# The values of an mLSTM as seven half-depth products, and which work fills which stage

## The chip, the cores and the metric

The kernel runs on one core of one Trainium2 chip. The metric is the device time of one execution in microseconds (us). A profile is one further execution, recorded by the hardware profiler; its times are us from the first instruction. The engines are TensorE (PE; its weight loads are PEld), VectorE (DVE), ScalarE (ACT), GpSimd (POOL) and SyncE (SP), which issues most DMAs.

## The reference, cut to what matters

One block of a model: x is 1024 rows of 1024 numbers, all arithmetic in float32. `h` is the normed x, and one big projection of it gives everything else.

```python
h = rmsnorm(x, norm_g[layer])
proj = jnp.einsum('bsd,de->bse', h, w_in[layer])
(a_q, a_k, a_v, a_o, a_z, a_g, b_q, b_k, b_v, b_z, g_a, g_b) = jnp.split(proj, _split_points(), axis=-1)
...
y_a = hm * jax.nn.sigmoid(a_o) * jax.nn.silu(a_z)
...
y_b = att.reshape(B, S, DA_WIDTH).astype(x.dtype) * jax.nn.silu(b_z)
mix = (jax.nn.sigmoid(g_a + gb[0]) * jnp.einsum('bsc,cd->bsd', y_a, w_branch_a[layer])
       + jax.nn.sigmoid(g_b + gb[1]) * jnp.einsum('bsc,cd->bsd', y_b, w_branch_b[layer]))
x = x + jnp.einsum('bsd,de->bse', mix, w_out[layer])
```

Each part of `proj` is 1024 wide, but for a_g, which is 16. `hm` comes from an mLSTM over four heads of 256 (q and k go through a short convolution and silu, the values a_v directly), run forward and backward. `att` is an attention over eight heads of 128, each the difference of two softmaxes.

## The kernel before, in words

**Precision.** Every product is made of float32r matmuls of split operands: each operand is a rounded high part H and the rest L, and HxH, HxL and LxH are summed, three matmuls per slice of 128 of the depth. For a weight block, `load_w` (L177) loads 512 KB into a `raw` tile (two of them), ScalarE copies it to `wH` (L204), and GpSimd subtracts to get `wL` (L209, or in eight pieces at L207 during the opening and the mLSTM). `run` (L386) lets these loads go ahead of use as far as six half-size weight slots allow.

**Pairs.** Two column blocks of w_in are multiplied together with Strassen-Winograd's scheme: seven products of half the depth in place of eight. The row combinations of h (`TH`, `TL`) are made once in the opening. `load_form` (L230) makes the seven combinations of weight quarters, `pair_units` (L270) the products, each with 512 columns moving and 12 matmuls; products 0, 1, 2 and 6 collect in bank X, 3 and 5 in G, 4 in F, and a `sink` takes each finished quarter. Sixteen pairs are done so: q and k of the mLSTM (`conv_sink`), and o and z of the mLSTM (`oz_sink`). The order in `build` lets product 6 and 5 of one pair stand among products 0, 3, 1, 4, 2 of the next. Large tiles of this stage are called `big` (six buffers), among them `cin`, `y` and `oz`; `tz` has two buffers.

**Units and filling.** Work is a list of units, each with a planned cost; `Weaver.weave` interleaves lists by cost and by the due times in `LAG`. TensorE's order is exactly that list (`keep(E.PE)`); behind the opening the other engines' and SP's instructions are placed by a scheduler. A gate (ga or gb, 16 blocks of 128 columns, each 48 matmuls in 16 units) depends on nothing and is used to fill: `fill(m)` takes the next m gates, and `gate_units` (L831) stores each finished half (tanh, L837, then a DMA to `tga` or `tgb`).

**Stages.**
1. Opening: x is loaded, normed and transposed; four gates fill.
2. The sixteen pairs.
3. Attention: for each of eight heads q and k with a rope (`da_proj`, L842), the head's z, and for two heads at once the values (`da_v`, L892, by `v_units`, L436). Scores of one of eight row blocks take two score tiles (L923); VectorE reduces each (L926), ScalarE takes the exponential (L928), VectorE combines them (L934); then transposes, the product with the values and a norm. `FILL` gives gates to heads 0 and 7. Three gates stand behind it.
4. mLSTM (`ml_head`, `ml_units` L1239): chunks of 256 rows, both directions. The values of head n+1 are projected by `v_units` as filler while head n runs, 32 units of six matmuls each; the first head's values stand ahead of it, the last head is filled with gates.
5. Behind the mLSTM `rest` holds the gates that are left. Five units of it go first, then the last outputs of the mLSTM (`late`) with some more, then loads of y of the attention (`load_y`, L1310: DMA to `yraw`, two buffers, ScalarE copy, VectorE subtraction, tile `sl_yb`) woven into what remains.
6. Products with w_branch_b (L1339), w_branch_a (L1341), then w_out (L1399).

The lines that set these counts:

```python
FILL = (1, 0, 0, 0, 0, 0, 0, 3)
...
ml, late = self.ml_units([self.ml_head(n, stm[n]) for n in range(NH_A)], fill(2))
...
rest = fill(len(gq))
cut = len(rest) // 4
w.add(*rest[:5])
w.weave(late, rest[5:cut])
```

Of the kernel before, what the change touches and what calls it, by code (L numbers as in the profile page):

```python
# [14 lines left out]
S = 1024  # L15
# [22 lines left out]
FILL = (1, 0, 0, 0, 0, 0, 0, 3)  # L38
# [71 lines left out]
class Block:  # L110
# [66 lines left out]
    def load_w(self, key, nxt=None):  # L177
# [3 lines left out]
        if key[0] == "sw":  # L181
            return self.load_form(key)
        wH = self.wpool.tile([128, 8, 128], F32R, name="wH", tag="wH")
# [35 lines left out]
    def pair_raws(self, p):  # L219
        if p >= len(self.pairs) or p in self.praws:  # L220
            return
        self.praws[p] = raws = []
        for seg, i in self.pairs[p]:
# [4 lines left out]
            raws.append(t)  # L228

    def load_form(self, key):  # L230
# [18 lines left out]
        elif f == 2:  # L249
            src = tmp("s3f")  # L250
            sub(src, r1[:, lo], r2[:, lo])
        elif f == 3:
            self.s1f = src = tmp("s1f")
# [16 lines left out]
    def pair_units(self, p, sink):  # L270
# [37 lines left out]
        return [[Unit(6 * MM, lambda f=f, k0=k0: product(f, k0), (("sw", p, f),)) for k0 in (0, 2)] for f in range(7)]  # L308

# [76 lines left out]
    def run(self, units):  # L386
# [10 lines left out]
        for i, u in enumerate(units):  # L397
            if u.keys:
# [4 lines left out]
                while nxt < len(order) and (order[nxt] in self.loaded or not self.opening  # L403
                                            and (order[nxt][0] != "sw" or hasattr(self, "_s0")) and ahead(order[nxt])):
# [436 lines left out]

    def da_proj(self, h, st):  # L842
# [44 lines left out]
        z = self.proj(kz, 0, lambda ps: zz(0, ps)) + self.proj(kz, 1, lambda ps: zz(1, ps), name=("z", h))  # L887
        for half in range(2):
            z[(half + 1) * self.PIECES - 1].after = ((("G", h - 1, half), LAG["G"]),)
# [138 lines left out]
    def ml_head(self, n, st):  # L1028
# [24 lines left out]
        def vv(c, ps):  # L1053


# [4 lines left out]
            a.copy(H[:, :, 0:DH], ps)  # L1060
            low(Lo[:, :, 0:DH], ps, H[:, :, 0:DH])
# [161 lines left out]
        def out(i, half):  # L1223
            ps = self.bank("T")
            for k in range(4):
# [8 lines left out]
                    v=self.v_units("av", n, vv, order=(3, 2, 1, 0)), weigh=step(weigh),  # L1234
# [4 lines left out]
    def ml_units(self, heads, gates):  # L1239
# [5 lines left out]
        av = list(x["v"])  # L1245
        take = lambda n: [av.pop(0) for _ in range(n)]
        for c in (3, 2, 1, 0):
            un += x["k"](c)
        for c in range(NC):
            un += x["gb"](c) + x["HL"](c)  # L1250
        un += take(12) + x["weigh"](3, 1) + take(4) + x["state"](3, 1)
        un += x["weigh"](2, 1) + take(6) + x["state"](2, 1)
        un += x["weigh"](1, 1) + take(6) + x["state"](1, 1) + x["split"](0)
        un += take(4) + x["S"](0) + gates[0:8]
        gates = gates[8:]
        prev = None
        for n, x in enumerate(heads):
            nx = heads[n + 1] if n + 1 < len(heads) else None
            if nx:
                other, share = list(nx["v"]), ((3, 3), (2, 1), (2, 2), (3, 3), (2, 2), (1, 2), (2, 1), (2, 1))  # L1260
            else:
                other, share = gates, ((2, 2), (1, 1), (2, 1), (2, 1), (2, 1), (2, 1), (2, 0), (1, 0))
            for t in range(8):
# [37 lines left out]
                if nx:  # L1301
                    un += {1: nx["k"](3) + nx["gb"](0), 2: nx["k"](0) + nx["k"](2) + nx["HL"](0), 3: nx["k"](1) + nx["gb"](1),
                           4: nx["HL"](1), 5: nx["gb"](2), 6: nx["HL"](2), 7: nx["gb"](3) + nx["HL"](3)}.get(t, [])
# [125 lines left out]
    def build(self):  # L1429
# [21 lines left out]
        with pool(name="const", bufs=1) as self.const, \  # L1451
# [20 lines left out]
            self.pairs, sinks, self.praws, self.f = [], [], {}, {}  # L1472
            for n in range(NH_A):
                for i, seg in enumerate(("ak", "aq")):
# [3 lines left out]
                    sinks.append(self.oz_sink(2 * n + i))  # L1478
            self.ident = self.const.tile([128, 128], F32, name="ident")
# [27 lines left out]
            g0, g1, g2, g3 = (fill(1) for _ in range(4))  # L1507
# [28 lines left out]
            products = [self.pair_units(i, sinks[i]) for i in range(len(self.pairs))]  # L1536
# [31 lines left out]
            ml, late = self.ml_units([self.ml_head(n, stm[n]) for n in range(NH_A)], fill(2))  # L1568
# [72 lines left out]
```

## Time and profile before

| | |
|---|---|
| Runs, median of 3 | 1688.82 us |
| Runs, lowest and highest | 1687.5 and 1688.95 us |
| Profiled execution, first to last instruction | 1685.6 us |
| Matmuls in the profile, transposes among them | 9431 |
| DMA over the span | 178.79 MB, 106 GB/s |
| Stage 1, 2, 3 (from, us) | 0, 71, 398 |
| Stage 4, 5, 6 (from, us) | 1108, 1377, 1413 |

The profiled execution's own time is its span, 3.2 us under the median of the runs. In the profile a group's mean duration of a matmul includes its passage through the array, so that matmuls overlap; what one costs in a stream is the spacing, the length of an unbroken stretch over the matmuls in it. A row with "<-" names who ended a wait. A row ending in q (SPq) is an engine's sequencer issuing.

### The profile page before, as it was taken

How to read it: one execution, taken by the hardware profiler on the slowest of the kernel's cores; microseconds unless marked ns; L12 is line 12 of the kernel's file. 1: busy time of each engine (PE TensorE's matmuls, PEld its weight loads, DVE VectorE, ACT ScalarE, POOL GpSimd, SP SyncE). 2: the span in 40 equal slices, each digit the busy share in tenths (PEclk: the TensorE clock that was granted, in tenths of full speed). 3: DMA queues.
4: the chain of work that ended last, by engine and by line, in shares of the span. 5: the costliest groups of instructions: out<-in, count | busy, mean ns of one | idle time of the engine just before them, and what ended most of it. 6: DMA issues, size and time to landing. Idle time of an engine off the chain costs nothing. (4 is left out here: it accounts for less than half of the span.)

```text
span 1685.6 us, 25370 instructions
## 1 busy us (share of the span) xinstructions
PE 1645.8 (98%) x9431; PEld 1385.3 (82%) x9431; DVE 992.4 (59%) x1799; ACT 760.3 (45%) x1522; POOL 635.2 (38%) x712
## 2 busy tenths in 40 slices
PE   7999999999999999999999999999999999999998
PEld 5777887887877988898888888899999877888887
DVE  5778678675286766666666665325666754135533
ACT  7454555553255454444445445334655644122221
POOL 5767676655343334333451332122322412212000
PEclk9999999999999999999999999999999999999999
DMA  5334434434231213211322222166455337344222
GB/s 180 101 117 137 138 113 137 126 125 127 74 80 48 74 38 88 51 51 39 100 59 56 62 58 70 57 181 176 144 160 161 89 117 244 126 149 126 88 93 83
DMA packets 175630, 178.79 MB, mean 106 GB/s; under 512 B 12185, under 2 KB 135410, under 8 KB 175506
## 3 DMA queue, kind: packets, MB, share of 16 engines
q1 hardware_dynamic: 174594, 175.58, 34.8%
q8 instruction: 74, 1.21, 0.3%
q10 hardware_dynamic: 912, 1.59, 0.2%
q14 instruction: 50, 0.41, 0.1%
HBM read 114.11 MB, written 46.24 MB: 95 GB/s over the span
## 5 line engine op out<-in xcount | busy, mean ns | idle before, releaser
L429 PE MATMUL pj<-hH,wH 128*128 128x512 f32 x640 | 265.8, 415 | 3.3 <-ACT f L542 1.5
L429 PE MATMUL pj<-hH,wL 128*128 128x512 f32 x640 | 251.3, 393 | 1.8 <-POOL wL L207 1.8
L429 PE MATMUL pj<-hL,wH 128*128 128x512 f32 x640 | 250.1, 391 | 0.2 <-DVE hL L580 0.2
L209 POOL TENSOR_TENSOR wL<-raw,wH 128x1024 fp32r<-128x1024 f32 x41 | 99.7, 2432 | 278.0 <-ACT wH L204 268.3
L928 ACT ACTIVATE e<-S,nm 128x1024 f32<-128x1024 f32 x128 | 142.7, 1115 | 134.1 <-DVE nm L926 133.9
L948 DVE TENSOR_TENSOR pL<-T,pH 128x512 fp32r<-128x512 f32 x128 | 87.9, 688 | 117.4 <-ACT pH L947 116.7
L926 DVE TENSOR_REDUCE nm<-S 128x1 f32<-128x1024 f32 x128 | 150.5, 1217 | 10.1 <-PE S L923 9.3
L451 PE MATMUL pj<-wH,hH 128*128 128x256 f32 x512 | 149.9, 293 | 1.6 <-DVE vL L1035 1.4
L429 PEld LDWEIGHTS pj<-hH,wH 128*128 128x128 f32 x640 | 120.4, 188 | 37.7 <-issue 14.1
L451 PE MATMUL pj<-wL,hH 128*128 128x256 f32 x512 | 144.9, 283 | 1.4 <-POOL wL L207 1.4
L429 PEld LDWEIGHTS pj<-hH,wL 128*128 128x128 f32 x640 | 120.1, 188 | 30.2 <-POOL wL L207 3.4
L451 PE MATMUL pj<-wH,hL 128*128 128x256 f32 x512 | 144.5, 282 | 0.0
L429 PEld LDWEIGHTS pj<-hL,wH 128*128 128x128 f32 x640 | 120.7, 189 | 18.2 <-DVE hL L580 0.6
L429 PE MATMUL pj<-sl_yb,wH 128*128 128x512 f32 x384 | 118.9, 390 | 2.1 <-DVE sl_mb L1339 1.6
L947 ACT CAST pH<-T 128x512 fp32r<-128x512 f32 x128 | 74.7, 584 | 100.5 <-PE T L131 99.8
L204 ACT CAST wH<-raw 128x1024 fp32r<-128x1024 f32 x56 | 58.8, 1050 | 114.7 <-PE pj L429 75.8
L923 PE MATMUL S<-kst,qq 64*128 64x512 f32 x768 | 106.5, 408 | 0.0
L451 PEld LDWEIGHTS pj<-wH,hH 128*128 128x128 f32 x512 | 97.7, 191 | 6.8 <-issue 3.9
L451 PEld LDWEIGHTS pj<-wL,hH 128*128 128x128 f32 x512 | 97.5, 190 | 2.3 <-POOL wL L207 2.3
L451 PEld LDWEIGHTS pj<-wH,hL 128*128 128x128 f32 x512 | 97.7, 191 | 0.1
L934 DVE SCALAR_TENSOR_TENSOR e<-e,r,e 128x1024 f32<-128x1024 f32 x64 | 88.9, 1389 | 2.2
L923 PEld LDWEIGHTS S<-kst,qq 64*128 64x128 f32 x768 | 67.8, 184 | 26.2 <-issue 10.5
(358 smaller groups left out, 4101.4 us busy)
## 6 DMA issues: line engine op xcount, KB each, us to landing
raw<-in_w_in_dram SPq DMA_DIRECT2D x88, 512.0 KB, 3.9
kst<-hl SPq DMA_DIRECT2D x64, 128.0 KB, 2.4
qq<-hl SPq DMA_DIRECT2D x64, 128.0 KB, 2.4
x<-in_x_dram SPq DMA_DIRECT2D x8, 512.0 KB, 6.2
cak<-y SPq DMA_DIRECT2D x16, 256.0 KB, 2.3
cakH<-cin SPq DMA_DIRECT2D x16, 256.0 KB, 4.4
cakL<-tz SPq DMA_DIRECT2D x16, 256.0 KB, 4.1
gm<-oz SPq DMA_DIRECT2D x16, 256.0 KB, 2.8
```

What stands on the lines that cost most here:

```text
L204: self.a.copy(wH, raw)
L209: self.p.tensor_tensor(out=wL, in0=raw, in1=wHf, op=ALU.subtract)
L429: self.t.matmul(ps, lhsT=l[:, k, :], rhs=r, start=(n == 0), stop=(n == 23))
L451: self.t.matmul(ps[:, i, :], lhsT=l, rhs=r[:, k, :], start=(kh == 0 and k == 0 and m == 0), stop=(kh == 1 and k == 3 and m == 2))
L923: self.t.matmul(ps[:, o], lhsT=qq[r, x, c], rhs=k[r, y, o], start=(m == 0), stop=(m == 2))
L926: v.tensor_reduce(out=nm, in_=ps, axis=AX.X, op=ALU.max, negate=True)
L928: a.activation(out=e, in_=ps, func=AF.Exp, bias=nm[:, 0:1], accum_out=Z[:, j, t:t + 1])
L934: v.scalar_tensor_tensor(out=e0, in0=e, scalar=r[:, 0:1], in1=e0, op0=ALU.mult, op1=ALU.add)
L947: a.copy(pH[:, :, s], ps)
L948: v.tensor_tensor(out=pL[:, :, s], in0=ps, in1=pH[:, :, s].bitcast(F32), op=ALU.subtract)
```

## The change

The values of the mLSTM get two pairs of their own, behind the sixteen others. One pair is two blocks of 256 columns of a_v, so the forms are [512 x 256], `wH` and `wL` of full size; here h moves to the stationary side and 256 weight columns stream. Each product is 4 row groups x 12 matmuls. `v_sink` splits each quarter and stores H and L in DRAM (`vd`); the mLSTM loads them where it projected before. The lower halves of the raw blocks and some temporaries lie in `big` tiles that are taken over (`kit`) near the end of the last narrow pair.

In return the mLSTM is filled with gates (`fill(9)`), and the opening makes z of heads 0, 1, 3 and 5 in place of four gates, stores it (`zd`), and the attention loads it. `FILL` is two gates in place of four, all in head 7. `rest` is thereby two gates, where it was three.

The diff, cut to its core:

```diff
-FILL = (1, 0, 0, 0, 0, 0, 0, 3)
+FILL = (0, 0, 0, 0, 0, 0, 0, 2)
+Z_EARLY = (0, 1, 3, 5)
...
+        if self.pairs[p][0] == "v":
+            pool = self.wpool if p % 2 == 0 else self.s0
+            for b in range(2):
+                t = pool.tile([128, 8, 128], F32, name="raw", tag="raw", **({} if p % 2 == 0 else dict(bufs=2)))
+                raws.append({0: wide(t)})
+                self.load_piece(p, b, 0)
...
+    def spare(self, n):
+        while len(self.kit) < n:
+            self.kit.append(self.big("kit")[:, 0:S])
+
+    def far_pieces(self, p, blocks=(1, 0)):
+        i = 0 if p % 2 == 0 else 4
+        for b in blocks:
+            self.praws[p][b][1] = self.kit[i + 1 - b].rearrange("p (k e) -> p k e", e=256)
+            self.load_piece(p, b, 1)
+
+    def load_wide_form(self, key):
...
+        elif f == 3:
+            self.s1w = src = s13
+            g.tensor_tensor(out=src, in0=r2[0], in1=r2[1], op=ALU.add)
...
+        a.copy(H, src)
+        (self.v if f in (0, 4, 6) else g).tensor_tensor(out=Lo, in0=src, in1=H.bitcast(F32), op=ALU.subtract)
...
+    def wide_units(self, p, sink):
...
+            for k in range(4):
+                for m, (l, r) in enumerate(((bH, wH), (bL, wH), (bH, wL))):
+                    self.t.matmul(ps, lhsT=l[:, k, c], rhs=r[:, k, :], start=(new and k == 0 and m == 0), stop=(k == 3 and m == 2),
+                                  skip_group_check=not new)
...
+        return [[Unit(12 * TP, lambda f=f, i=i: product(f, i), (("sv", p, f),)) for i in range(4)] for f in range(7)]
+
+    def v_sink(self, g):
+
+        def sink(i, j, b, ps, rest):
+            t = lambda: self.s0.tile([128, 512], F32, name="tz", tag="tz", bufs=2)
+            if rest is not None:
+                to = self.psA.tile([128, 512], F32, name="pj", tag="pj", bufs=2) if i == j == 1 else ps
+                self.v.tensor_tensor(out=to, in0=ps, in1=rest, op=ALU.add)
+                ps = to
+            H, Lo = t(), t() if rest is None else rest
+            self.a.copy(H.bitcast(F32R), ps)
+            self.v.tensor_tensor(out=Lo.bitcast(F32R), in0=ps, in1=H, op=ALU.subtract)
+            for x, y in (("H", H), ("L", Lo)):
+                self.q.dma_start(out=self.vd[x][2 * g + i][2 * j + b], in_=y)
+        return sink
...
+    def z_units(self, h):
+
+        def done(half, ps):
+            t = self.wpool.tile([128, 512], F32, name="gt", tag="gt")
+            self.a.copy(t, ps)
+            self.a.dma_start(out=self.zd[h][:, half * 512:(half + 1) * 512], in_=t)
...
+        if h in Z_EARLY:
+            z = [Unit(0.0, lambda half=half: load(half), name=("z", h) if half else None) for half in range(2)]
...
+        def load_v(c):
             k = c if n % 2 == 0 else (2, 1, 0, 4)[c]
             H, Lo = st["v", c] = tuple(w2.tile([128, NB, DH + 2], F32R, name=f"v{y}", tag=f"v{y}{k}", bufs=1) for y in "HL")
             p.memset(H[:, :, DH:DH + 2].bitcast(F32), 1.0)
             p.memset(Lo[:, :, DH:DH + 2].bitcast(F32), 0.0)
-            a.copy(H[:, :, 0:DH], ps)
-            low(Lo[:, :, 0:DH], ps, H[:, :, 0:DH])
+            for x, y in (("H", H), ("L", Lo)):
+                q.dma_start(out=y[:, :, 0:DH].bitcast(F32), in_=self.vd[x][n][c].rearrange("p (b e) -> p b e", b=NB))
...
-        un += take(12) + x["weigh"](3, 1) + take(4) + x["state"](3, 1)
-        un += x["weigh"](2, 1) + take(6) + x["state"](2, 1)
-        un += x["weigh"](1, 1) + take(6) + x["state"](1, 1) + x["split"](0)
-        un += take(4) + x["S"](0) + gates[0:8]
-        gates = gates[8:]
+        un += take(8) + x["weigh"](3, 1) + take(3) + x["state"](3, 1)
+        un += x["weigh"](2, 1) + take(5) + x["state"](2, 1)
+        un += x["weigh"](1, 1) + take(4) + x["state"](1, 1) + x["split"](0)
+        un += take(4) + x["S"](0)
...
-                other, share = list(nx["v"]), ((3, 3), (2, 1), (2, 2), (3, 3), (2, 2), (1, 2), (2, 1), (2, 1))
+                other, share = take(32), ((3, 3), (2, 1), (2, 2), (3, 3), (2, 2), (1, 2), (2, 1), (2, 1))
...
-            g0, g1, g2, g3 = (fill(1) for _ in range(4))
+            g0, g1, g2, g3 = (self.z_units(h) for h in Z_EARLY)
...
+            products[fv - 1][2].insert(0, do(lambda: (self.spare(5), self.far_pieces(fv))))
+            products[fv - 1][5].append(do(lambda: (self.spare(6), self.far_pieces(fv + 1))))
...
-            ml, late = self.ml_units([self.ml_head(n, stm[n]) for n in range(NH_A)], fill(2))
+            ml, late = self.ml_units([self.ml_head(n, stm[n]) for n in range(NH_A)], fill(9))
```

More of the change, by code (lines that the diff above doesn't have):

```diff
@@ L839, in gate_units @@
         return sum((self.proj(key, half, lambda ps, half=half: done(half, ps)) for half in range(2)), [])
+    def z_units(self, h):
[3 more added lines that the diff above has]
+            self.a.dma_start(out=self.zd[h][:, half * 512:(half + 1) * 512], in_=t)
+        key = ("w_in", OFF["bz"] + 128 * h)
+        return sum((self.proj(key, half, lambda ps, half=half: done(half, ps)) for half in range(2)), [])
     def da_proj(self, h, st):
@@ L1478, in build @@
                     sinks.append(self.oz_sink(2 * n + i))
+            self.first_v = len(self.pairs)
+            for g in range(2):
+                self.pairs.append(("v", "av", g))
+                sinks.append(self.v_sink(g))
             self.ident = self.const.tile([128, 128], F32, name="ident")
```

113 lines of the change are left out of this document (99 added, 14 removed).

## The prediction

> **What bounds the kernel now.** I read the page first, then the waits of TensorE, then busy time by stretches, then the chain that ended last.
>
> ```profile
> span 1685.6 us, 25370 instructions
> PE 1645.8 (98%) x9431; PEld 1385.3 (82%) x9431; DVE 992.4 (59%) x1799; ACT 760.3 (45%) x1522; POOL 635.2 (38%) x712
> PEclk9999999999999999999999999999999999999999
> ```
>
> TensorE is busy for 98% at full clock: 39.8 us of the span are idle, and the rest only shrinks if there are fewer matmuls. Fewer matmuls are a gain only where TensorE doesn't then wait for something else. Where it waits today:
>
> ```profile
> PE T L291 <- ACT u L298: 3.2, 4, 1.2
> PE pj L429 <- DVE sl_mb L1339: 1.6, 1, 1.6
> PE pj L451 <- POOL wL L207: 1.4, 4, 0.5
> PE pj L429 <- DVE zg L881: 1.4, 1, 1.4
> PE pj L451 <- DVE vL L1035: 1.4, 1, 1.4
> ```
>
> The columns are the total wait, how often, and the longest. No stage has a large wait, so each is held by its matmuls. That says nothing of how near the next engine is. The stretches show that (columns: length, then busy time and count for PE, PEld, DVE, ACT, POOL):
>
> ```profile
> 71.00:398.00 327.00, 322.17 (x1392) 255.11 (x1393) 239.55 (x363) 173.12 (x312) 217.94 (x195) 1.00 0.41 127
> 455.30:518.10 62.80, 62.80 (x375) 49.85 (x374) 47.29 (x63) 32.91 (x65) 25.67 (x22) 1.00 0.31 81
> 597.40:675.90 78.50, 78.50 (x465) 63.49 (x464) 52.20 (x72) 37.61 (x81) 33.08 (x33) 1.00 0.26 68
> 1211.00:1386.00 175.00, 165.05 (x1240) 153.47 (x1240) 115.39 (x414) 104.30 (x261) 43.93 (x107) 1.00 0.41 125
> ```
>
> They are the sixteen pairs, attention head 0, attention head 2, and most of the mLSTM. In head 0 VectorE already has 47.29 of 62.80 us.
>
> **The products.** Before, the values take 4 heads x 32 units x 6 = 768 matmuls of 256 columns, half of the 1536 of line 451. After, they take 2 pairs x 7 products x 4 x 12 = 672 of the same shape. Their spacing, and that of the 512-column matmuls of line 429, where they run unbroken:
>
> ```profile
> 432.30:455.30 23.00, 23.00 (x192) 1.00 0.20 47
> 1384.20:1413.40 29.20, 29.20 (x129) 1.00 0.87 285
> ```
>
> That is 23.00/192 = 0.120 us and 29.20/129 = 0.226 us. 96 matmuls fewer save **11.5 us**. The gates and z keep their number. A gate or a z is 48 matmuls of 0.226 = 10.9 us, and these only move: four z from the attention into the opening (where four gates leave), seven gates more in the mLSTM, two fewer in the attention, and **one fewer behind the mLSTM** (the remaining list goes from three gates to two).
>
> **The tail behind the mLSTM.** This last move is the important one. The remaining gates are TensorE's work while y of the attention (8 tiles `yraw<-yb`) is loaded and split for the first product with w_branch_b. The chain that ended last runs through these loads:
>
> ```profile
> 1387.25 0.32 SPq L838
> 1387.69 4.26 DMA yraw<-yb
> 1394.62 0.96 ACT sl_yb L1314
> 1395.60 2.64 DVE sl_yb L1315
> 1398.26 4.01 DMA yraw<-yb
> 1402.30 1.06 ACT sl_yb L1314
> 1403.39 1.24 DVE sl_yb L1315
> 1404.64 4.04 DMA yraw<-yb
> 1411.04 4.64 DMA yraw<-yb
> 1415.70 1.06 ACT sl_yb L1314
> 1416.79 1.23 DVE sl_yb L1315
> ```
>
> Two `yraw` buffers let one load follow only when the subtraction two loads earlier is done. The eighth tile is ready at 1416.79 + 1.23 = 1418.0. TensorE begins the product here:
>
> ```profile
> 1413.49 0.61 PE L429 MATMUL pj<-sl_yb,wH 128*128 128x512 f32 x2
> ```
>
> Its eighth slice of depth is 21 matmuls later, at 1413.5 + 4.75 = 1418.2: just in time. After the change 27 of the 43 units behind the first five are left, 81 matmuls in place of 129, so TensorE arrives 48 x 0.226 = 10.9 us sooner, at 1407.3 on the same scale. The loads start behind the store of the first remaining half gate (1387.25, unit 8) and behind the last mLSTM outputs, and both stand where they stood. If the chain is unchanged TensorE waits 10.7 us. At best each round takes 4.0 + 1.06 + 1.24 + 0.07 = 6.4 us, four rounds from 1388.1 end at 1413.7, and it waits 6.4. I take **+8.5**, the middle: one copy `wH`, one tanh and one long subtraction lie in the first round today, and they are instructions that stay.
>
> Why the subtraction took 2.64 us and not 1.24 is seen beside it:
>
> ```profile
> 1394.75 2.40 POOL L209 TENSOR_TENSOR wL<-raw,wH 128x1024 fp32r<-128x1024 f32 x1 [13.03 <-ACT wH L204]
> ```
>
> GpSimd's ended at 1397.15, and VectorE's was done 1.1 us later. The Trainium skill ("SBUF — State Buffer", section "SBUF: two separate sides") says that a VectorE operation with two SBUF inputs and a GpSimd one that reads SBUF exclude each other for a whole instruction; the trace agrees with 2.64 against 1.24 us. By this rule the wide forms, with GpSimd busier, could each hold up a VectorE subtraction by up to 2.4 us, and the sum would be 0 to 2 us higher.
>
> **The two wide pairs.** Per pair GpSimd has eight operations of 128x1024, ScalarE seven copies of them, VectorE three subtractions:
>
> ```profile
> L209 POOL TENSOR_TENSOR wL<-raw,wH 128x1024 fp32r<-128x1024 f32 x41 | 99.7, 2432 | 278.0 <-ACT wH L204 268.3 <-DMA raw<-in_w_branch_b_dram 7.3 <-PE T L291 2.4
> L204 ACT CAST wH<-raw 128x1024 fp32r<-128x1024 f32 x56 | 58.8, 1050 | 114.7 <-PE pj L429 75.8 <-issue 15.4 <-POOL hl L869 13.1
> raw<-in_w_in_dram SPq DMA_DIRECT2D x88, 512.0 KB, 3.9
> cakL<-tz SPq DMA_DIRECT2D x16, 256.0 KB, 4.1
> ```
>
> 8 x 2.43 = 19.5 us of GpSimd and 7.4 us of copies lie beside 336 x 0.120 = 40.3 us of matmuls, so the engines suffice. One form takes 2.43 + 1.05 + 2.43 = 5.9 us and is begun two products (11.5 us) ahead, except at the seam to the narrow pairs, where it has one wide and one narrow product (about 5.8 + 2.9 = 8.7 us). Each sink keeps a `tz` tile until its store lands (4.1 us); product 6 asks for four of the two within 5.8 us, so ScalarE and a bank wait about 1 us, once per pair. I take **+2.0**; bounds 0 (all hidden) and 7 (the second rival). SP gets 32 more stores of 256 KB here (8.4 MB over 80 us, 105 GB/s, beside the 127 GB/s that this stage has).
>
> **The attention.** Heads 2, 4 and 6 lose a z, head 7 a gate: 78.5 - 10.9 = 67.6 us against VectorE's 52.2 in head 2, still covered. Head 0 loses its only gate: 62.8 - 10.9 = 51.9 us, and VectorE's 47.29 is 91% of that. The next scores need both score tiles free:
>
> ```profile
> L926 DVE TENSOR_REDUCE nm<-S 128x1 f32<-128x1024 f32 x128 | 150.5, 1217 | 10.1 <-PE S L923 9.3
> L928 ACT ACTIVATE e<-S,nm 128x1024 f32<-128x1024 f32 x128 | 142.7, 1115 | 134.1 <-DVE nm L926 133.9
> L934 DVE SCALAR_TENSOR_TENSOR e<-e,r,e 128x1024 f32<-128x1024 f32 x64 | 88.9, 1389 | 2.2
> ```
>
> Two reductions and an exponential, 2.43 + 1.12 us behind the scores' own matmuls, are well under the 6.5 us that one of eight steps keeps, but VectorE has the 1.39 and two subtractions as well. Bounds 0 and 4, I take **+1.5**. Four z now come by eight loads on SP, queued behind the `kst`/`qq` copies that wait for GpSimd; the tanh behind them is needed only at the head's end, so nothing waits. z[0] no longer stands between head 0's queries and values; the 23.0 us of the value products still cover the rope chain.
>
> **The mLSTM.** Its fill becomes 144 units of gates of 0.68 us (three of 0.226) where it had 128 units of values of 0.72 (six of 0.120) and 32 of gates; the 96 and the last 24 fall on the same steps as before, the first part shrinks from 40 units to 24. The 8 x 256 KB of values of the first head are queued on SP ahead of its q and k parts: at the 285 GB/s of the tail's row they take 7.4 us. The last of the first chunk's parts is issued, and its scores begin, here:
>
> ```profile
> 1117.95 0.94 SPq L1046 DMA_DIRECT2D aqL<-caqL  x2
> 1138.21 0.28 PE L127 MATMUL SS<-akH,aqH 128*128 128x256 f32 x1
> ```
>
> That is a lead of 20.3 us. The loads come 7.4 us later, and the scores 6.7 us sooner, since 24 units of gates stand ahead of them (16.3 us) where 32 of values stood (23.0). 6.2 us are left, for a landing of about 3. For later heads `v` loads wait for a slot whose reader (`PO`) has run, and the next chunk's parts stand behind them on SP; these are not used before the next head. **+0.5**, bounds 0 and 4.
>
> **Waits that go.** 1.4 (zg), 1.4 (vL) and two of 0.5 (wL of the values) belong to what is removed or moved, 3.8 in all. Behind the first, value banks are late next. I take **-2.5**; bounds -3.8 and 0.
>
> **Sum:** -11.5 - 2.5 + 8.5 + 2.0 + 1.5 + 0.5 = -1.5, span 1684.1. The median of the runs is 3.2 us over the profiled span, so **1687.3**. The opening is the same work (z by a copy instead of a tanh).
>
> **The clock.** The longest waits that I expect in the tail are 2 to 4.5 us each, between tiles 4, 5, 6 and 7. The Trainium skill ("TensorE: Matmul & The Clock Gate", section "HAM oscillation — how this bites in real kernels") says that idle gaps over about 3.4 us halve the clock; no run here shows it, since the longest of the waits quoted above is 1.6 us. By it the product behind the gap would run at half speed for one window, an estimate of 1.7 us lost, and the sum would be 1689.0.
>
> **Rivals.** *Tail hidden anyway:* the scheduler may issue the `yraw` loads ahead of the gate's store, or the rounds shorten. For it: SP's order is not fixed by the program. Against: tile by tile the chain is limited by its two buffers, and a start 10 us sooner would lie ahead of the mLSTM outputs whose memory it takes. Without the 8.5 it gives 1678.8.
>
> *Slower, a late half block:* form 3 of the first wide pair needs the lower half of its second block, which goes into a buffer handed over by the last convolution pair. If its load is issued behind that pair's stores, it starts here:
>
> ```profile
> 395.83 0.80 SPq L383 DMA_DIRECT2D caqL<-y  x1
> 391.30 0.50 PE L291 MATMUL T<-TH,wH 128*128 128x512 f32 x1 [0.68 <-ACT u L298]
> ```
>
> The load then begins at 396.2 and the form is done at 396.2 + 3.9 + 5.9 = 406.0. TensorE stands at 390.6 before the wide product 0 (the second row is what follows today) and reaches product 3 at 390.6 + 8.7 = 399.3, so it waits 6.7 us. It decides from a load issued after 389.5. With the other terms 1694.0.
>
> **Chances.** Forecast 0.60 (its own range 1682 to 1691.5), tail hidden 0.17, late half 0.23. Range 1679.0 to 1695.5: from the first rival to the second with some of the other bounds. 0.2% is 3.4 us, about what can be told from no change. Faster: 0.17 and a third of 0.60, 0.36. Slower: most of 0.23 and little of the rest, 0.22. Same: 0.42.
>
> **What would show it.** Right: 96 matmuls of 256 columns fewer; waits of line 429 for `sl_yb` totalling 6 to 11 us where the first w_branch_b product begins; head 0 near 53 us; the wide pairs near 82 us. Wrong: no wait there (first rival), or one of over 5 us before product 3 of the first wide pair (second). If the mLSTM waits for `v` loads, my lead of 6.2 us was wrong.

## The result, and the profile after

| | before | after |
|---|---|---|
| Runs, median of 4 | 1688.16 us | 1724.9 us |
| Runs, lowest and highest | 1685.98 and 1688.95 us | 1723.74 and 1725.98 us |
| Profiled execution, span | 1685.6 us | 1724.2 us |

The ratio is 1.022, with a 95% interval of 1.0206 to 1.0235. The change makes the kernel 2.2% slower, and the forecast of 1687.3 us, with its range up to 1695.5, was wrong.

The page of the kernel after, the lines that answer to those of before:

```profile
span 1724.2 us, 25403 instructions
PE 1653.9 (96%) x9335; PEld 1385.9 (80%) x9335; DVE 1015.4 (59%) x1817; ACT 776.8 (45%) x1548; POOL 661.2 (38%) x713
PEclk9999999998999999999999999998999998999999
```

The 96 matmuls are gone (9431 to 9335). Yet TensorE is busy for 8.1 us more, not for 11.5 less. Its idle time grew from 39.8 to 1724.2 - 1653.9 = 70.3 us. So the 38.6 us of span are 30.5 us of new waits and 8.1 us of slower matmuls. The three 8s in PEclk say where to look for the second part.

From the list of TensorE's waits in the kernel after (line, who ended them, total us, how often, longest):

```profile
PE pj L558 <- ACT gt L966: 11.9, 1, 11.9
PE pj L558 <- ACT sl_yb L1457: 4.7, 3, 2.8
PE T L132 <- ACT att L1107: 3.5, 5, 1.1
PE T L401 <- DVE wL L288: 3.5, 1, 3.5
PE T L128 <- ACT kwH L1225: 3.4, 4, 2.8
PE T L401 <- POOL wL L288: 3.1, 1, 3.1
PE T L401 <- ACT wH L287: 2.6, 1, 2.6
PE pj L580 <- DVE hl L1002: 2.2, 1, 2.2
PE pj L558 <- DVE sl_yb L1458: 2.1, 5, 0.8
PE S L1069 <- ACT e L1074: 1.7, 2, 1.1
```

One wait of 11.9 us stands out, then three in the wide products (L401, 9.2 us together), and those for y of the attention (`sl_yb`, 6.8 us). Of all these the list of the kernel before has only two: the one for `kwH` with 0.5 us, and the last but one with 0.4 us.

Stretches of the kernel after in which the granted clock was low (length, busy time and count of PE, PEld, DVE, ACT, POOL, then PEclk, the share of DMA and GB/s):

```profile
395.00:399.00 4.00, 4.00 (x24) 4.00 (x23) 2.71 (x4) 2.15 (x4) 1.78 (x2) 0.58 0.61 142
409.00:416.00 7.00, 5.48 (x25) 5.48 (x26) 1.38 (x2) 2.19 (x4) 7.00 (x4) 0.52 0.00 0
522.00:526.00 4.00, 4.00 (x23) 4.00 (x22) 0.00 (x0) 0.00 (x0) 3.94 (x6) 0.58 0.02 4
590.00:597.00 7.00, 6.40 (x28) 5.28 (x28) 4.75 (x7) 3.52 (x7) 0.44 (x2) 0.51 0.44 102
1173.00:1178.00 5.00, 4.98 (x19) 4.04 (x18) 1.80 (x4) 0.62 (x1) 0.00 (x0) 0.66 0.81 237
1184.00:1195.00 11.00, 3.74 (x11) 3.04 (x12) 0.00 (x0) 0.69 (x1) 0.00 (x0) 0.53 0.87 270
1423.00:1427.00 4.00, 4.00 (x15) 3.30 (x14) 1.57 (x3) 0.00 (x0) 0.00 (x0) 0.57 1.01 355
1450.00:1461.00 11.00, 6.94 (x15) 4.17 (x16) 4.37 (x4) 2.96 (x4) 0.00 (x0) 0.53 0.62 204
```

In each row the busy time times the share that the clock lacks is what slow matmuls cost: 4.00 x 0.42 = 1.7, 5.48 x 0.48 = 2.6, and so on, 17.6 us in all. With one more such stretch in the opening (1.6) it makes 19.2 us, and -11.5 + 19.2 explains 7.7 of the 8.1 us. The kernel before has no such stretch but in its last microseconds. The first two stand behind the waits of the wide products, the third at the start of the attention, the fourth in its head 0, the fifth behind the wait for `kwH`, the sixth around the long one, the last among those for `sl_yb`.

By stage, from the starts of the same instructions in both traces. "Matmuls alone" is the time before plus or minus the matmuls that the change adds or takes there, at 0.120 and 0.226 us (in the mLSTM's first head also the eight gate units that stood in it, 5.4 us):

| Stage (us) | before | matmuls alone | after | lost |
|---|---|---|---|---|
| opening and pairs | 398.0 | 478.6 | 489.7 | 11.1 |
| start of the attention | 57.3 | 46.4 | 50.6 | 4.2 |
| head 0 | 62.8 | 51.9 | 59.0 | 7.1 |
| heads 2, 4, 6 together | 235.5 | 202.8 | 207.3 | 4.5 |
| head 7 to the mLSTM's first scores | 146.6 | 129.0 | 134.1 | 5.1 |
| mLSTM, first head | 60.9 | 54.2 | 67.5 | 13.3 |
| mLSTM, second and third head | 123.0 | 120.4 | 116.4 | -4.0 |
| last mLSTM output to half of the first w_branch_b product | 42.9 | 32.0 | 42.7 | 10.7 |

Heads 1, 3 and 5 take 79.3 us in both. The rows lose 52.0 us together. The span is 50.1 us over what the matmuls alone would give (1685.6 - 11.5 = 1674.1), so the stretches that are not listed gave 1.9 us back.

**The long wait.** SP's issues in the kernel after, from the last stores of gates ahead of the mLSTM on:

```profile
1152.44 0.32 SPq L967 DMA_DIRECT2D tgb<-gt  x1
1152.80 0.61 SPq L1205 DMA_DIRECT2D vH<-avH  x1
...
1159.98 0.53 SPq L1205 DMA_DIRECT2D vH<-avH  x1
1160.55 0.61 SPq L1205 DMA_DIRECT2D vL<-avL  x1
1161.20 1.07 SPq L1197 DMA_DIRECT2D gb<-gg  x2
...
1185.50 1.71 SPq L1192 DMA_DIRECT2D aqL<-caqL  x2
1187.38 0.32 SPq L967 DMA_DIRECT2D tgb<-gt  x1
1187.79 0.38 SPq L174 DMA_DIRECT2D raw<-in_w_in_dram  x1
```

And ScalarE's tanh of the gates in the same time, then TensorE behind it:

```profile
1156.45 0.69 ACT L966 ACTIVATE gt<-pj,gbh 128x512 f32<-128x512 f32 x1 [4.04 <-PE pj L558]
1190.52 0.69 ACT L966 ACTIVATE gt<-pj,gbh 128x512 f32<-128x512 f32 x1 [14.78 <-DMA tgb<-gt]
```
```profile
1191.26 0.80 PE L558 MATMUL pj<-hH,wH 128*128 128x512 f32 x1 [11.91 <-ACT gt L966]
1191.85 0.63 PE L558 MATMUL pj<-hL,wH 128*128 128x512 f32 x1
1192.27 0.63 PE L558 MATMUL pj<-hH,wL 128*128 128x512 f32 x1
...
1196.27 0.39 PE L558 MATMUL pj<-hH,wH 128*128 128x512 f32 x1
1196.49 0.40 PE L558 MATMUL pj<-hL,wH 128*128 128x512 f32 x1
```

Read from the end: TensorE needs a `pj` bank, which the tanh of the next half gate must empty. The tanh needs the only `gt` tile, which the store of the half gate before must free. That tile was full at 1156.45 + 0.69 = 1157.1, but its store was issued at 1187.38, 30 us later: on SP's queue all loads of the mLSTM's first head, the new ones of the values among them, were issued ahead of it, the last at 1185.50. Behind the wait the matmuls are spaced by 0.43 us and, 5 us later, by 0.22.

### The profile page after: what moved, and what is told of

It is laid out like the page before. It is cut to its first block, busy times and chain, and to the rows that moved or that the text cites. A ratio compares the mean times of both kernels' runs of the same rounds, so it can differ in the third digit from the quotient of the medians.

```text
span 1724.2 us, 25403 instructions
## 1 busy us (share of the span) xinstructions
PE 1653.9 (96%) x9335; PEld 1385.9 (80%) x9335; DVE 1015.4 (59%) x1817; ACT 776.8 (45%) x1548; POOL 661.2 (38%) x713
## 5 line engine op out<-in xcount | busy, mean ns | idle before, releaser
L558 PE MATMUL pj<-hH,wH 128*128 128x512 f32 x640 | 270.0, 422 | 13.9 <-ACT gt L966 11.9
L1074 ACT ACTIVATE e<-S,nm 128x1024 f32<-128x1024 f32 x128 | 142.5, 1115 | 98.0 <-DVE nm L1072 97.9
L212 POOL TENSOR_TENSOR wL<-raw,wH 128x1024 fp32r<-128x1024 f32 x34 | 82.7, 2433 | 235.4 <-ACT wH L207 235.4
L207 ACT CAST wH<-raw 128x1024 fp32r<-128x1024 f32 x48 | 50.4, 1051 | 107.0 <-PE pj L558 89.8
L558 PEld LDWEIGHTS pj<-sl_yb,wH 128*128 128x128 f32 x384 | 73.2, 191 | 25.8 <-ACT sl_yb L1457 6.2
L356 PE MATMUL T<-TH,wH 128*128 128x512 f32 x256 | 86.9, 398 | 1.1 <-ACT u L363 1.1
L502 DVE SCALAR_TENSOR_TENSOR pj<-cin,cols,pj 128x512 f32<-128x512 f32 x128 | 87.1, 747 | 1.1 <-ACT pj L500 1.1
L356 PE MATMUL T<-TH,wL 128*128 128x512 f32 x256 | 86.2, 398 | 1.4 <-ACT u L363 1.1
L132 PE MATMUL T<-ident,e 128*128 128x128 f32 x512 | 77.0, 273 | 5.4 <-ACT att L1107 3.5
L580 PE MATMUL pj<-wH,hH 128*128 128x256 f32 x256 | 75.8, 296 | 3.1 <-DVE hl L1002 2.2
```

Of the source, the lines that this page charges most:

```text
L132: self.t.transpose(out, in_, self.ident[0:k, 0:k])
L212: self.p.tensor_tensor(out=wL, in0=raw, in1=wHf, op=ALU.subtract)
L356: self.t.matmul(ps, lhsT=l[:, k, :], rhs=r[:, k, :], start=(first and k == 0 and m == 0), stop=(k == 3 and m == 2), skip_group_check=not f ...
L502: v.scalar_tensor_tensor(out=acc, in0=raw[:, o + x:o + x + 512], scalar=w(x), in1=acc, op0=ALU.mult, op1=ALU.add)
L558: self.t.matmul(ps, lhsT=l[:, k, :], rhs=r, start=(n == 0), stop=(n == 23))
L580: self.t.matmul(ps[:, i, :], lhsT=l, rhs=r[:, k, :], start=(kh == 0 and k == 0 and m == 0), stop=(kh == 1 and k == 3 and m == 2))
```

## The experiments

The theory (A): the loss is the sum of several new waits, each from work that was moved, and of the clock that they cost. Its rivals in the various runs are other causes for the same wait, or none at all. The runs were made on several chips, and the kernel before, run beside each group of them, had medians from 1687.5 to 1690.0 us; so two runs are told apart by their ratios, and medians that are 2 us or less apart say little. Long lines of the edits are cut, which "..." marks.

| Run | Median, us | Ratio to before, 95% interval | Span | PE busy | Clock |
|---|---|---|---|---|---|
| before | - | 1 | 1685.6 | 1645.8 | 0.999 |
| after | 1724.9 | 1.0206 to 1.0235 | 1724.2 | 1653.9 | 0.984 |
| gate stores by ScalarE | 1720.04 | 1.0165 to 1.0197 | 1718.4 | 1652.9 | 0.987 |
| first values' loads by ScalarE | 1722.86 | 1.0179 to 1.0211 | 1720.2 | 1651.7 | 0.986 |
| early half block | 1716.76 | 1.0137 to 1.0173 | 1715.7 | 1650.7 | 0.986 |
| three gates behind the mLSTM | 1718.95 | 1.0155 to 1.0189 | 1718.8 | 1650.6 | 0.988 |
| a gate for head 0 | 1721.81 | 1.0188 to 1.0218 | 1721.0 | 1652.3 | 0.985 |
| z of head 0 later | 1725.06 | 1.021 to 1.0241 | 1726.1 | 1653.7 | 0.984 |
| first wide `wL` by GpSimd | 1723.93 | 1.0182 to 1.024 | 1720.5 | 1651.9 | 0.985 |
| five of these together | 1705.16 | 1.0091 to 1.0121 | 1703.8 | 1646.7 | 0.993 |
| other z early, with three of them | 1701.62 | 1.0068 to 1.0098 | 1698.7 | 1643.3 | 0.995 |
| other z early alone | 1726.88 | 1.0214 to 1.0248 | 1725.0 | 1653.4 | 0.984 |
| before, fewer value matmuls | 1684.76 | 0.9975 to 0.9993 | 1683.1 | 1642.9 | 0.996 |
| before, two short gates | 1680.36 | 0.9946 to 0.9974 | 1678.6 | 1633.5 | 0.997 |

**The gate stores go to ScalarE's queue.**

```diff
-(self.a if self.opening else self.q).dma_start(out=self.tg[seg][i] ...
+(self.a if self.opening or self.ml else self.q).dma_start(out=self.tg[seg][i] ...
```

> Gates that fill the mLSTM store their halves through ScalarE's queue in place of SP's, nothing else. Theory A (a store stuck on SP): the 11.9 us wait of TensorE behind the first mLSTM scores (gt L966) comes from the first gate half's store, which stands on SP behind some 45 loads and holds the one gt tile, so that the next half's tanh and its PSUM bank wait. Then the wait falls under 1 us, the slowed clock beside it goes, and the run is 12 to 15 us shorter: about 1711. Theory B (traffic): the added 2 MB of value loads make the first head's inputs late, and the bank is only where it shows. Then the loads are as late as before, the wait moves to the first scores or states, and the run gains under 4 us.

The wait of 11.9 us is gone, so its cause is the store on SP's queue. The first and second head of the mLSTM in this kernel:

```profile
1179.70:1234.30 54.60, 53.80 (x358) 48.38 (x358) 33.23 (x129) 30.23 (x75) 12.91 (x36) 1.00 0.87 265
1234.30:1295.20 60.90, 58.11 (x386) 51.65 (x385) 39.57 (x144) 35.98 (x91) 16.23 (x41) 1.00 0.74 219
```

The first head takes 54.6 us in place of 67.5, what its matmuls alone take (54.2). But the span fell by 5.8 us only, and the median by 4.9 where 12 to 15 were expected. The next heads take 60.9 and 59.7 us where they took 58.2, the stretch that loads y of the attention is 1.1 us longer, and the lead of the first head 1.7. The repair is real, and 7 of the 12.9 us that the first head gains are given back elsewhere. It may be that TensorE comes earlier to the next late input and waits there; no run takes this apart.

**The first head's value loads go to ScalarE's queue**, the store stays on SP.

```diff
-q.dma_start(out=y[:, :, 0:DH].bitcast(F32), in_=self.vd[x][n][c] ...
+(a if n == 0 else q).dma_start(out=y[:, :, 0:DH].bitcast(F32), in_=self.vd[x][n][c] ...
```

> The value loads of the first mLSTM head are issued on ScalarE's queue in place of SP's; the bytes are the same and the gate stores stay on SP. Theory A: SP reaches the store about 5 us sooner (eight issues of 0.6 us), so the 11.9 us wait shrinks to about 7, and the 2.8 us wait for kwH goes, since gb is loaded sooner: 7 to 9 us shorter. Theory B (the value loads themselves are the cause): both waits go, 14 us shorter or more.

Waits of TensorE in this run:

```profile
PE pj L558 <- ACT gt L966: 5.9, 1, 5.9
PE T L128 <- issue: 3.7, 1, 3.7
```

The store is issued at 1181.59 us in place of 1187.38, and half of the wait goes with the eight loads; the other half is from the loads of q, k and the gates' rows, which still stand ahead of it. The wait for `kwH`, which was expected to go, stays at 2.9 us, and a new wait of 3.7 us ahead of the same head's first scores takes back more than half of the gain. The median is 2.0 us lower in place of 7 to 9, and the interval of the ratio overlaps that of the kernel after.

**The lower half block is loaded earlier**: the second block's, which form 3 needs, at the last narrow pair's product 0 instead of 2.

```diff
+products[fv - 1][0].insert(1, do(lambda: (self.spare(1), self.far_pieces(fv, (1,)))))
-products[fv - 1][2].insert(0, do(lambda: (self.spare(5), self.far_pieces(fv))))
+products[fv - 1][2].insert(0, do(lambda: (self.spare(5), self.far_pieces(fv, (0,)))))
```

> The first wide pair's lower half of the second block gets its buffer one pair earlier (during the last narrow pair), so that its load is not behind the last convolution pair's stores; nothing else. If the late load is the cause of the waits before product 3 (2.6 and 3.2 us), both go and the run is 6 to 8 us shorter (the slowed clock goes with them); the 3.5 us before product 0, which waits for VectorE's subtraction, stays. If GpSimd's queue is the cause, the waits stay within 1 us and the run is unchanged.

The pairs end at 480.9 instead of 489.7; two of the three waits of the wide products are gone, and 3.5 us (`wL L288`) stay. The median is 8.1 us lower, as expected. So the late half block, the second rival of the prediction, is shown to be the cause of these two waits. In the kernel after three loads into `kit` tiles were issued from here on, the first of them this half block, the only one that form 3 needs. GpSimd began form 3 6.0 us behind that issue:

```profile
397.42 5.18 SPq L246 DMA_DIRECT2D kit<-in_w_in_dram  x3
```
```profile
403.39 2.35 POOL L279 TENSOR_TENSOR s<-raw,kit 128x1024 f32<-128x1024 f32 x1 [6.43 <-issue]
405.81 2.35 POOL L264 TENSOR_TENSOR kit<-s,raw 128x1024 f32<-128x1024 f32 x1
408.12 2.34 POOL L288 TENSOR_TENSOR wL<-s,wH 128x1024 fp32r<-128x1024 f32 x1
```

The last row is the `wL` of form 3, for which TensorE waits 3.1 us. The row before it belongs to form 1, which GpSimd took first. TensorE's wait for form 3's copy `wH` ended at 406.87, so the subtraction could have begun there; it began at 408.12, and 1.25 of the 3.1 us are from this order.

**The first wide `wL` is made by GpSimd**, since VectorE made it late, behind the last convolution's work.

```diff
-(self.v if f in (0, 4, 6) else g).tensor_tensor(out=Lo, in0=src, ...
+(self.v if f in (4, 6) or f == 0 and p > self.first_v else g).tensor_tensor(out=Lo, in0=src, ...
```

> The subtraction of the first wide pair's product 0 runs on GpSimd, which is idle there, in place of VectorE, which has the last convolutions in front of it. The 3.5 us wait before product 0 goes or falls under 1 us. The late half block still sets product 3, which waits until the same moment: then the gain of 3.5 is taken up there and the run is unchanged within 1 us; if the two waits add up, 3.5 us shorter.

The pairs end 3.3 us earlier and the wait of 3.5 is gone, but the copy behind it is waited for longer (`wH L287`, 4.4 us where it was 2.6). The span is 3.7 us shorter, but the median only 1.0 us lower, inside what can be told.

**Three gates behind the mLSTM**, one in head 7.

```diff
-FILL = (0, 0, 0, 0, 0, 0, 0, 2)
+FILL = (0, 0, 0, 0, 0, 0, 0, 1)
```

> One gate goes from attention head 7 to the list behind the mLSTM, which has three gates again. My account of the tail: the waits for sl_yb (6.4 us in sum) and the slowed clock there go, head 7 is 10.9 us shorter with no new wait over 1 us, and the run is 8 to 10 us shorter. Rival: the loads are simply slower beside the heavier traffic of the mLSTM, and the gate is missed in head 7, whose VectorE then binds: under 3 us.

The waits for `sl_yb` by ScalarE are gone; a wait of 3.3 us for the other y (`sl_mb`) comes. The stretch behind the last mLSTM output takes 44.8 us with 10.9 us of matmuls more, where it took 42.7: there the gate costs 2.1. Head 7 with the mLSTM's lead is 7.1 us shorter, not 10.9, so 3.8 us of what was taken there had been cover (time in which TensorE would otherwise have waited). The median is 6.0 us lower, where 8 to 10 were expected.

**A gate for head 0**, one in head 7.

```diff
-FILL = (0, 0, 0, 0, 0, 0, 0, 2)
+FILL = (1, 0, 0, 0, 0, 0, 0, 1)
```

> One gate moves from attention head 7 to head 0, nothing else. Theory A (heads bound by what follows the scores where too little fill is left): head 0, 59 us for 52 of planned matmuls, becomes 63 with 10.9 us more work, so 7 us come back there; head 7 and the end behind it give back 7 us for a gate of 10.9, as they did when a gate was moved behind the mLSTM, so 4 are lost there; in sum 3 us shorter, 1722. Theory B (the heads are bound by matmuls and the slow clock only): both stages move by 10.9 and the run is unchanged.

Head 0 takes 62.9 us in place of 59.0: 10.9 us of work for 3.9. Head 7 gives 5.6 of 10.9. Together 3.2 us of span, about what was expected; but the interval of the ratio overlaps that of the kernel after.

**The early z of head 0 is taken up later**, behind the first values.

```diff
-w.add(..., *qk[0], *z[0], *self.da_v(0, sts[0:2]))
+w.add(..., *qk[0], *self.da_v(0, sts[0:2]), *z[0])
```

> The early z of head 0 is loaded and worked on behind the first value products in place of ahead of them, nothing else. If VectorE's z operation, which waits for its load, holds up the rope operations behind it on VectorE, the waits at the attention's start (0.4, 1.0 and 2.2 us) go and the run is 3 to 4 us shorter. If the waits come from the buffers that the pair stage hands over, they stay and the run is unchanged.

Nothing came of it: the start of the attention takes 50.2 us, and TensorE still waits 2.2 us for `hl`. So the loaded z does not hold up the rope chain; what does was not found.

**Five together**: the stores on ScalarE's queue, the early half block, the first `wL` by GpSimd, z later, and `FILL = (1, 0, 0, 0, 0, 0, 0, 0)` with three gates behind.

> All together: gate stores on ScalarE's queue in the mLSTM, the early half block, the subtraction on GpSimd, z of head 0 behind the values, and the gates of head 7 moved to head 0 and behind the mLSTM (three there). If the waits are separate causes, the measured gains add (5.9 + 8.2 + 3.5 + 3.5 + 6 + 3): 1695, less what head 7 loses without any gate (3 to 4): 1695 to 1699, still slower than before the change. If they share a cause (traffic, the clock), under 20 us come back: 1705 or more.

20.4 us of span come back, and the median, 1705.16, is the one that was expected if the waits share a cause, not the 1695 to 1699 of separate causes. What they share was not found; that each repair alone was partly taken back later (see the first) fits it as well as traffic would. The pairs now end at 477.9, with nothing lost against the matmuls alone. Head 7 and the mLSTM's lead hold most of what stays: 128.3 us for 107.2 us of matmuls (129.0 less two gates).

**Another choice of z**, to give heads 0 and 7 cover without a gate.

```diff
-Z_EARLY = (0, 1, 3, 5)
+Z_EARLY = (1, 2, 3, 5)
-nxt = fill(FILL[h]) + z[h]
+nxt = z[h - 1] + fill(FILL[h]) + z[h]
-nxt = z[h - 1] + ahead + fill(FILL[h]) + z[h] if h else ahead + fill(FILL[0])
+nxt = z[h - 1] + ahead + (z[h] if h < 6 else []) if h else ahead + z[0]
```

z of head 0 no longer stands ahead of the first values. With the first three repairs of "five together" and three gates behind the mLSTM, one in head 7:

> All five repairs, but the cover of heads 0 and 7 now comes from z and not from gates: z of heads 1, 2, 3 and 5 is made in the opening, z of head 0 is woven into head 0 and z of head 6 into head 7; one gate stays in head 7, three behind the mLSTM. Theory A (what the five repairs together still lose is TensorE without cover in head 7, where 128.4 us now pass for about 112 us of matmuls, and in front of the mLSTM): heads 2 and 6 fall from 69 to about 59 us, head 7 with the lead of the mLSTM stays at 128 to 132 us though it has 21.8 us of matmuls more, head 0 stays at 63; the median 1687 to 1693, about 14 below the five repairs. Rival B (what is left is lost to the 8.4 MB written and 8.4 MB read again, and to VectorE in every head): heads 2 and 6 stay above 65 us, and the median stays above 1700.

And alone:

> The changed kernel with that other choice of z alone (z of heads 1, 2, 3 and 5 in the opening, z of head 0 in head 0, z of head 6 in head 7; two gates in head 7 and two behind the mLSTM as changed). Theory A: head 0 at 62.8 us, heads 2 and 6 at about 59, head 7 with the lead at about 140; the wait for the gate's tanh at the mLSTM's first chunk, the waits of the wide pairs and those for y of the attention stay; about 9 us shorter, median near 1716. Rival B: no difference, 1722 to 1726.

Alone it gains nothing, as the rival had it. Head 0 takes 62.8 us as before the change, and head 7 with the lead 145.2. But heads 2 and 6, which gave up the z, take 66.4 and 62.7 us and not 59, where their matmuls alone take 56.7. With the repairs it has the lowest median, though its interval overlaps that of the five, and it is still 0.7 to 1.0% slower than the kernel before. It was expected at 1687 to 1693 with heads 2 and 6 near 59 us; the median over 1700 and head 2 over 65 us are what the rival said (values written and read again, and VectorE in every head), head 6 is not. Heads 2 and 6 of that version:

```profile
667.00:734.50 67.50, 61.32 (x369) 48.18 (x368) 50.93 (x69) 36.08 (x77) 28.53 (x30) 0.95 0.31 83
962.20:1024.90 62.70, 59.53 (x369) 47.13 (x368) 50.55 (x68) 35.10 (x73) 27.09 (x27) 0.97 0.32 85
```

TensorE idles for 6.2 and 3.2 us and loses clock as well. Its longest waits in head 2 are for ScalarE (`T` L1117, 2.9 us once, and `e` L1074, 1.7 us in two); in neither head does it wait for a DMA itself, and VectorE is busy for 50.93 of the 67.5 us. So neither the traffic nor VectorE is shown to be what is left. The whole version's PE busy time, 1643.3, is 2.5 under that of the kernel before; its idle time, 55.4, is 15.6 over it, and the sum is the 13.1 us of span by which it is longer.

**The kernel before with 96 matmuls fewer.** If the waits are mended and the kernel is still slower, is the saving itself worth what it was taken for? This leaves out one slice of depth in the mLSTM's values.

```diff
-for k in range(k0, k0 + 2):
+for k in range(k0, k0 + 2 - (seg == "av" and kh == 0 and k0 == 2)):
```

> The kernel before, but the values of the mLSTM leave out one of their eight slices of depth: 96 of 768 matmuls of 256 columns, the number that the seven products save, and nothing else is changed (so the values are computed in part only). Theory A (the saving itself is real, and is lost again by what is moved to make it): close to 11.5 us shorter, at least 8; median 1676 to 1680. Rival B (TensorE's matmuls in and before the mLSTM are only cover for other chains, so that taking any away changes nothing): less than 4 us shorter, 1684 to 1688.

It is 2.5 us shorter in span and 0.16% in time (0.07 to 0.25%), not 11.5: in the kernel before these matmuls are not worth their time. TensorE in this kernel, as the second head begins:

```profile
1198.37 0.28 PE L451 MATMUL pj<-wH,hL 128*128 128x256 f32 x1
1198.49 0.28 PE L451 MATMUL pj<-wL,hH 128*128 128x256 f32 x1
1199.82 0.39 PE L451 MATMUL pj<-wH,hH 128*128 128x256 f32 x1 [1.05 <-ACT wH L204]
1200.04 0.28 PE L451 MATMUL pj<-wH,hL 128*128 128x256 f32 x1
1200.82 0.38 PE L451 MATMUL pj<-wL,hH 128*128 128x256 f32 x1 [0.50 <-POOL wL L207]
...
1201.66 0.39 PE L451 MATMUL pj<-wL,hH 128*128 128x256 f32 x1 [0.21 <-POOL wL L207]
...
1205.19 0.41 PE L127 MATMUL SS<-akH,aqL 128*128 128x256 f32 x1
1205.40 0.41 PE L451 MATMUL pj<-wH,hH 128*128 128x256 f32 x1
```

TensorE comes 2.9 us sooner (24 matmuls) and waits 1.05 us for the copy of a weight block that had been in time; the other two waits were there before, with the same lengths. Three short waits within 3 us are then followed by matmuls spaced by 0.21 us in place of 0.12, for 3.4 us. The head takes 61.4 us, as before (61.5). Three such pieces of slow clock, in the second, the third and the last head, are 5.1 of the 9.0 us that are missing.

This is a finding on the kernel before. The change takes all these matmuls out of the mLSTM and puts gates there, and its second and third head took 4.0 us less than by their matmuls; how much of the 11.5 it could have kept, no run shows.

**The kernel before with two short gates**, one in head 0 and one behind the mLSTM. Each leaves out 36 of its 48 matmuls; its loads, its tanh and its stores stay.

```diff
+if key in self.short and 0 < n // 3 < 7:
+    continue
```

> The kernel before, but the gate that fills attention head 0 and the last gate behind the mLSTM leave out six of their eight slices of depth: 36 of 48 matmuls each, 8.1 us each; their weights are still loaded, and their tanh and their stores are still made (so these two gates are computed in part only). Theory A (there the gates are cover, and TensorE waits for other engines when they go): head 0 takes 58 to 60 us and not 54.7, the stretch from the last mLSTM output to half of the first w_branch_b product shrinks from 42.9 by 0 to 2.5 us, and the median is 3 to 7 us lower, 1681 to 1685. Rival B (each matmul taken away is time): both stretches 8.1 us shorter, the median near 1672.

As the theory had it. Head 0 takes 58.2 us, 4.6 less for 8.1 us of matmuls. The stretch behind the mLSTM takes 41.6 us where it took 42.9, 1.3 less for 8.1; first the kernel before, then this one:

```profile
1383.20:1426.10 42.90, 41.33 (x185) 33.91 (x185) 16.13 (x14) 17.32 (x20) 7.34 (x3) 1.00 0.83 266
```
```profile
1377.90:1419.50 41.60, 36.49 (x149) 28.91 (x150) 16.20 (x14) 17.39 (x20) 7.25 (x3) 0.92 0.82 273
```
```profile
1404.80 0.80 PE L431 MATMUL pj<-sl_yb,wH 128*128 128x512 f32 x1 [3.76 <-ACT gt L839]
```

This row is the longest new wait, at the start of the product with w_branch_b. It is for the tanh of the gate's last half, which frees the bank. On ScalarE this tanh stands at 1404.07, behind the copy of a weight block and a copy of y that waited 0.88 us for its load. So TensorE is stopped here by ScalarE's order as well as by the loads of y; whether another order would have saved more was not tried.

## Why the prediction was wrong

**The saving, -11.5.** The 96 matmuls are gone as computed, and the wide pairs cost their 80.6 us once they hardly wait (they end at 477.9 in the five repairs, where the matmuls alone give 478.6). But the prediction took matmuls for time wherever they leave: "No stage has a large wait, so each is held by its matmuls". A stage without waits can as well be one whose other chains end just in time, as the prediction itself warned; a busy share of 98% does not tell the two apart. The short values of the kernel before give 2.5 us for the same number of matmuls. Set against the terms of the sum, the table's losses are: attention 15.8 us (4.2 + 7.1 + 4.5) for +1.5, mLSTM with its lead 14.4 (5.1 + 13.3 - 4.0) for +0.5, wide pairs 11.1 for +2.0, tail 10.7 for +8.5.

**"These only move."** This is the step that failed most: what was moved, gates and z, was costed as 48 matmuls, both where it left and where it came. In the mLSTM it failed by what a gate brings along. A gate also has a tanh, a store on SP's queue and one `gt` tile. The prediction looked at what the value loads delay (the q and k parts) and found 6.2 us of lead, which held: no wait for these parts is in the list. It did not look at what else was behind them on SP. In place of "+0.5 mLSTM" the first head lost 13.3 us, 11.9 of it this wait; moving the store away took it off, which shows the cause. Ahead of it the lead lost 5.1 us. TensorE's wait there, and ScalarE's work before it, in the kernel after:

```profile
1172.67 0.39 PE L128 MATMUL T<-vH,kwH 128*128 128x258 f32 x1 [2.79 <-ACT kwH L1225]
```
```profile
1171.35 0.91 ACT L1282 ACTIVATE W<-W,gc_negM 128x256 f32<-128x256 f32 x2 [2.43 <-POOL W L1280]
1172.17 0.45 ACT L1225 ACTIVATE kwH<-T,gc_ws 128x256 fp32r<-128x256 f32 x1
```

The weighed k (`kwH`) was behind an exponential that waited for GpSimd; with fewer fill units between, it seems, TensorE was there first. 2.8 us of wait and 1.7 of slow clock (1173 to 1178) are most of the 5.1; no run took this wait away.

**The wide pairs, +2.0.** The second rival happened: the late half block, priced there at 6.7 us of wait. Measured were 9.2 us of waits, 3.5 of them before the loads mattered (the first `wL` stood on VectorE behind the convolution), and 11.1 with the clock. The rival had the load begin at 396.2 and land 3.9 us later; it was issued at 397.42, and GpSimd began the form 6.0 us behind that. The 1.25 us that form 1 cost in between were not in the rival's 5.9 us for a form either.

**The attention, +1.5, "nothing waits".** Head 0 lost 7.1 us, over the upper bound of 4. The bound came from the time of single instructions; the short gate of the kernel before shows that 8.1 us of matmuls there are worth 4.6. In the kernel after TensorE is busy for 55.6 of head 0's 58.9 us, where it had no idle time before; its waits there are for ScalarE (`e` L1074, 1.7 us, and `att` L1107, 1.1), and the slow clock of the fourth stretch costs 3.1 us. At the start of the attention 4.2 us were lost: TensorE waits 2.2 us for `hl` when z of head 0 no longer stands there, so "the 23.0 us of the value products still cover the rope chain" was wrong. No run of the changed kernel removes this wait. The slow clock behind it (522 to 526) is 1.7 us more. In heads 2, 4 and 6 TensorE idles for about 1 us each.

**The tail, +8.5.** Right in its mechanism: 10.7 lost, 6.8 as waits for `sl_yb` and 3.3 in the last low stretch of the clock, of which the prediction had the first. The prediction's bounds were 6.4 and 10.7.

**The waits that go, -2.5.** Those for `zg`, `vL` and the values' `wL` are gone from the list. Their place was taken by others.

**The clock.** It was priced at 1.7 us in one place, and it cost 19.2. The sum treated each of its six terms by itself, and several waits were paid for twice, once as idle time and once as slow matmuls.

What stays open: the version with the lowest median is 13.1 us longer than the kernel before, and 24.6 longer than its matmuls would have it. 10.8 and 6.0 of these stand in heads 2 and 6; the rest is spread in pieces of 1 to 3 us and was not taken apart. The second and third head of the mLSTM took less than the matmuls' sum in the kernel after (58.2 us each); TensorE's idle time there fell from 2.3 to 0.9 us in each, which is 2.8 of the 4.0 us, and the rest is open. Whether the 8.4 MB of values that are written and read again slow other transfers was not tested either.

## What to carry to other kernels

Before counting a saved matmul as time, ask of its stage what would be late if TensorE came there sooner; the quick test is to leave a part of those matmuls out of the kernel as it is and time that. When work is moved, list every instruction that goes with it, and for each its queue and its buffer: a small store behind a stage's loads, with one tile behind it, stopped TensorE for 11.9 us. A wait on TensorE can cost more than its length: in the kernel after, 30.5 us of new waits came with 19.2 us of slow clock.

## What the runs showed of the hardware

The granted clock falls to half in pieces of about 3.4 us: 0.57 over 4 us and 0.66 over 5 us both lack 1.7 us, 0.52 over 7 us lacks 3.4, and in the kernel with fewer value matmuls it is 0.50 from 1202.3 to 1205.7 us. The Trainium skill ("TensorE: Matmul & The Clock Gate", sections "HAM oscillation — how this bites in real kernels" and Part 1) gives just such a window, 3.4 us at half rate, and the trace agrees in that. In the first of these sections it gives as the rule that idle gaps over about 3.4 us bring it on. Here less is enough: waits of 1.05, 0.50 and 0.21 us within 3 us were followed by 3.4 us at half clock, and in the kernel before the 0.50 and the 0.21 alone were not. Nor does every wait bring it on: the single one of 1.6 us for `sl_mb` in the kernel before was followed by matmuls at full clock (1.00 from 1424.7 to 1430.0 us). The measurement decides: waits that are short but close together can cost the clock as well, 1.7 us for each piece in which TensorE is busy. How much idle time it takes was not measured by a run of its own.
